# SwiGLU blocks of a two-layer trunk: seven block products moved from the down projection to gate and up, and the down projection's products placed among those of the next chunks

## The chip, the core and the metric

The kernel runs on one core of a Trainium2 chip. TensorE (PE) multiplies into PSUM; VectorE (DVE) and ScalarE (ACT) do the elementwise work and read PSUM; GpSimd (POOL) here issues the DMAs that add to what lies in SBUF; SP issues the plain loads. The metric is the device time of one execution in microseconds. The kernel before takes 2116.01 us, the median of three runs (2115.99 to 2117.65).

## The reference, cut to what matters

The program is a decoder trunk of two layers for 512 tokens and a model width of 1024, in float32. Each layer has a SwiGLU half-step, a group of four mixers between an input and an output projection, a second SwiGLU half-step and a per-layer embedding (PLE) gate.

```python
def swiglu(x, w_gate, w_up, w_down):
    return (jax.nn.silu(x @ w_gate) * (x @ w_up)) @ w_down
...
for l in range(DEPTH):                       # DEPTH = 2, D_MODEL = 1024, D_FF = 2816, SEQ = 512
    h = h + 0.5 * swiglu(rmsnorm(h, ffn1_norm[l]), ffn1_w_gate[l], ffn1_w_up[l], ffn1_w_down[l])
    z = rmsnorm(h, mix_norm[l]) @ w_in[l]
    ...
    h = h + jnp.concatenate([y_a, y_b, y_c, y_d], axis=-1) @ w_out[l]
    h = h + 0.5 * swiglu(rmsnorm(h, ffn2_norm[l]), ffn2_w_gate[l], ffn2_w_up[l], ffn2_w_down[l])
    h = h + (p[l] @ ple_w_proj[l]) * jax.nn.sigmoid(rmsnorm(h, ple_norm[l]) @ ple_w_gate[l])
```

So there are four SwiGLU blocks. The change lies in them and in the stages that feed them.

## The kernel before, in words

**Layout.** Everything is held transposed: the residual `h` is 8 tiles of 128 features by 512 tokens (T), and a product's result has its output features on the 128 partitions. The hidden width 2816 is 22 chunks of 128. The weights lie in HBM so that the 8 blocks (128x128) of one output chunk are one row of 1024 columns.

**Products in float32.** Each float32 operand is split into a high part, rounded to the format fp32r, and a low part, the remainder. `parts` (L133) does it: ACT writes the high part, DVE subtracts. `weights` (L138) loads a row of 1024 columns and splits it; `split` (L201) splits an activation, with the norm's gain as a factor where there is one. `mm3` (L177) then does three matmuls for each 128x128 block: high by high, high by low, low by high. All large products go through it, so their matmuls have the lines L179 to L181 and are told apart by the tile they write.

**Norms.** `Norm.add` (L269) takes one finished tile of `h`: it splits gain times `h` into `x[k]` and adds the squares to `acc`. The row factor r = 1/sqrt(mean square) is made later by `scale` (L282) and multiplied in after the products, so that matmuls can begin before r is there.

**A SwiGLU block** is `ffn` (L296). `hidden` (L304) computes one chunk: the gate's and the up projection's product, each of 8 blocks by 512 tokens (48 matmuls for both, tiles `gu`), then g = silu(gate r) times up times r/2. The 22 chunks come in groups, `PARTS = (8, 8, 6)` (L50).

After each group of 8 comes `down7` (L322), which multiplies the group's 8 chunks by the down weights in the manner of Winograd's form of Strassen's method. The 8 output tiles are 4 pairs (i, i + 4); for each pair the left side is 2x2 (two output tiles by two halves of four chunks) and the right side 2x2 (two halves of four chunks by two halves of 256 tokens). Seven products of four 128x128 blocks by 256 tokens take the place of eight. The right-hand combinations are the tiles `hb1` to `hb4`, made as the chunks come. The left-hand ones are made by `seven` (L149) for each pair: four plain loads on SP's queue and two loads on POOL's queue that add to what the first brought (L163, L164), two sums on DVE (L168, L171), and seven splits of 512 columns. The results stand in the PSUM tiles `dx`, `dy` and `dz` and are added to `h` piece by piece (L365). The order of the 28 products is written out by hand (L368).

The last 6 chunks of a block are multiplied plainly (L384 to L388, tiles `dn`), output tile by output tile, and each finished tile goes to the next norm by `done`.

**Order and buffers.** A scheduler orders each engine's instructions by priority and readiness; work under `urgent` stands far ahead of its place in the program, which is how weights are loaded and split ahead of use. Buffers are slots of a tag: 6 of split weights (`w`), 3 of raw rows (`raw`), 4 of `side` (the sums in `seven`), 4 of `st`, 6 of `t` (temporaries of 128x512), 24 of `u` (pairs of 128x512), and in PSUM 4 `d` (`dense`) and 4 `m` (`mps`).

**The start.** The first chunk's weights and `x` come in pieces (L1060 to L1068), the second chunk's weights in halves (L1070 to L1079); the products of the first chunk are made as the pieces land.

**The stages ahead of a block.** The mixers' output projection (L953 to L960, tiles `y`) and PLE (`ple`, L962, tiles `pg` and `pp`) finish the tiles of `h` in the order 0 to 7 and hand each to `Norm.add`.

## Time and profile before

| | |
|---|---|
| median of three runs | 2116.01 us (2115.99 to 2117.65) |
| the profiled execution, its own time | 2118.98 us |
| its span, first to last instruction | 2117.2 us |
| mean granted TensorE clock | 0.997 |
| moved by DMA | 224.66 MB, 106 GB/s on average |

Where PE's time lies, by the tile that the matmuls write (groups by form, first of the three lines of `mm3`):

| tile | what | matmuls per line | columns |
|---|---|---|---|
| gu | gate and up | 1408 | 512 |
| dx, dy, dz | seven-product downs | 512, 256, 128 | 256 |
| dn | plain downs | 192 | 512 |
| z, n | input projection | 320, 128 | 512 |
| y | output projection | 128 | 512 |
| pg | PLE's gate | 96 and 64 | 512 and 256 |

How to read it: matmuls are pipelined, and the duration of one as the trace gives it (391 ns for 512 columns) is longer than the time from its start to the next one's start. What a matmul costs when PE is full is the length of a window divided by the number of matmuls in it. In the tables of windows the columns are the length, then for each engine its busy time and in brackets the number of its instructions, then the granted clock, the busy share of the DMA engines and GB/s; instructions that reach over an edge are counted in. A line of groups gives line, engine, operation, tiles, shapes and count, then the busy time and the mean ns of one, then the engine's idle time ahead of them and what ended it.

The blocks lie in the trace as follows: the first from 8.5 to 377 us, the second from 652.6 to 1007.3, the third from 1062.5 to 1416.6, the fourth from 1692.1 to 2046.5. Within the first, gate and up of chunks 0 to 7 end at 110.7, the first `down7` at 151.3, chunks 8 to 15 at 238.3, the second `down7` at 278.9, chunks 16 to 21 at 344.2.

### The profile page before, as it was taken

Reading aid. Unit: us, or ns where it says so; the run is one execution under the profiler, and the core shown is the slowest. Engines: PE = TensorE matmul, PEld = TensorE weight load, DVE = VectorE, ACT = ScalarE, POOL = GpSimd, SP = SyncE. Lnnn points to the kernel's source line nnn. Section 1 sums busy time; section 2 is a strip of 40 time slices with the busy share of each in tenths; the row PEclk is TensorE's granted clock in tenths of the full one; section 3 lists DMA queues with packets and bytes.
Section 4 is the critical chain, followed back from the end, with each engine's and each line's share of the span. In section 5 each row is a group of like instructions: output and inputs, shape, how many; then the busy total and the mean of one; then the engine's idle time right before and its main releaser. Section 6 shows DMA issues by size and latency. Waiting matters only on the chain.

```text
span 2117.2 us, 30818 instructions
## 1 busy us (share of the span) xinstructions
PE 2090.1 (99%) x12392; PEld 1755.5 (83%) x12392; DVE 1387.9 (66%) x2286; ACT 883.6 (42%) x1379; POOL 77.0 (4%) x109
## 2 busy tenths in 40 slices
PE   7999999999999999999999999999999999999997
PEld 5898988877788898988888989888777888889887
DVE  5695845786675675845767567467866658566476
ACT  5333423625644333424544333345445434243352
POOL 0010100001000000100000000000010000000000
PEclk9999999999999999999999999999999999999999
DMA  5353423322232453533234434232222335433241
GB/s 183 105 155 118 120 100 90 100 77 79 70 105 95 116 143 100 148 109 92 100 104 134 127 109 115 83 106 93 66 90 72 103 98 137 123 103 116 84 129 50
DMA packets 79376, 224.66 MB, mean 106 GB/s; under 512 B 9472, under 2 KB 13056, under 8 KB 79232
## 3 DMA queue, kind: packets, MB, share of 16 engines
q1 hardware_dynamic: 66320, 200.98, 29.1%
q0 software_dynamic: 10240, 18.88, 5.8%
q10 hardware_dynamic: 2672, 2.82, 0.4%
q8 instruction: 97, 1.59, 0.3%
q14 instruction: 47, 0.39, 0.1%
HBM read 218.45 MB, written 2.10 MB: 104 GB/s over the span
## 4 chain that ended last, share of the span: by engine, by line
PE 93%; DVE 3%; ACT 1%; DMA 1%; issue 1%; SPq 0%; DVEq 0%; ACTq 0%; POOLq 0%
PE gu L179 15%; PE gu L180 15%; PE gu L181 15%; PE z L179 3%; PE z L180 3%; PE z L181 3%; PE dx L179 3%; PE dx L180 3%; PE dx L181 3%; PE dn L179 2%; PE dn L180 2%; PE dn L181 2%; PE dy L181 1%; PE dy L179 1%; PE dy L180 1%; PE y L179 1%
## 5 line engine op out<-in xcount | busy, mean ns | idle before, releaser
L134 ACT CAST wh<-wr 128x1024 fp32r<-128x1024 f32 (+3 forms) x307 | 307.9, 1004 | 717.4 <-issue 330.7
L179 PE MATMUL gu<-x,wh 128*128 128x512 f32 x1408 | 550.3, 391 | 9.9 <-ACT wh L134 3.6
L180 PE MATMUL gu<-x,wh 128*128 128x512 f32 x1408 | 550.4, 391 | 0.0
L181 PE MATMUL gu<-x,wl 128*128 128x512 f32 x1408 | 550.0, 391 | 0.0
L135 DVE TENSOR_TENSOR wl<-wr,wh 128x1024 fp32r<-128x1024 f32 (+3 forms) x307 | 356.8, 1163 | 57.8 <-ACT wh L134 53.8
L179 PEld LDWEIGHTS gu<-x,wh 128*128 128x128 f32 x1408 | 265.7, 189 | 67.4 <-ACT wh L134 4.9
L180 PEld LDWEIGHTS gu<-x,wh 128*128 128x128 f32 x1408 | 265.9, 189 | 55.6 <-DVE x L209 0.6
L181 PEld LDWEIGHTS gu<-x,wl 128*128 128x128 f32 x1408 | 265.8, 189 | 55.0
L317 DVE TENSOR_TENSOR g<-g,gu 128x512 f32<-128x512 f32 x88 | 60.4, 688 | 256.9 <-PE gu L181 251.8
L179 PE MATMUL dx<-hb,ws 128*128 128x256 f32 x512 | 144.2, 285 | 0.3 <-ACT hb L134 0.3
L180 PE MATMUL dx<-hb,ws 128*128 128x256 f32 x512 | 144.3, 283 | 0.0
L181 PE MATMUL dx<-hb,ws 128*128 128x256 f32 x512 | 144.2, 283 | 0.0
L134 ACT CAST ws<-wr 128x512 fp32r<-128x512 f32 x128 | 78.5, 619 | 138.3 <-PE dx L181 84.5
L315 DVE TENSOR_TENSOR g<-gu,r 128x512 f32<-128x512 f32 x88 | 60.6, 689 | 103.0 <-PE gu L181 102.9
L179 PE MATMUL z<-x,wh 128*128 128x512 f32 x320 | 127.7, 399 | 0.0
L180 PE MATMUL z<-x,wh 128*128 128x512 f32 x320 | 126.6, 396 | 0.0
L181 PE MATMUL z<-x,wl 128*128 128x512 f32 x320 | 126.1, 394 | 0.0
L179 PEld LDWEIGHTS dx<-hb,ws 128*128 128x128 f32 x512 | 97.4, 191 | 2.0 <-ACT hb L134 0.5
L180 PEld LDWEIGHTS dx<-hb,ws 128*128 128x128 f32 x512 | 98.0, 191 | 0.3
L181 PEld LDWEIGHTS dx<-hb,ws 128*128 128x128 f32 x512 | 98.1, 192 | 0.0
L134 ACT CAST hb<-g 128x256 fp32r<-128x256 f32 (+1 forms) x128 | 58.8, 459 | 93.6 <-DVE g L318 45.1
L135 DVE TENSOR_TENSOR ws<-wr,ws 128x512 fp32r<-128x512 f32 x128 | 87.5, 689 | 11.4 <-ACT ws L134 11.2
(358 smaller groups left out, 3638.2 us busy)
## 6 DMA issues: line engine op xcount, KB each, us to landing
wr<-in_wgu SPq DMA_DIRECT2D x172, 512.0 KB, 3.2
wr<-in_winT SPq DMA_DIRECT2D x40, 512.0 KB, 3.2
s<-in_wdn SPq DMA_DIRECT2D x64, 256.0 KB, 3.8
s<-in_wdn POOLq DMA_DIRECT2D x64, 256.0 KB, 4.2
wr<-in_wdn SPq DMA_DIRECT2D x32, 512.0 KB, 3.6
wr<-in_wdn SPq DMA_DIRECT2D x32, 384.0 KB, 3.1
a<-in_wdn SPq DMA_DIRECT2D x32, 256.0 KB, 4.7
wr<-in_winN SPq DMA_DIRECT2D x16, 512.0 KB, 3.3
```

What stands on the lines that cost most here:

```text
L134: i = act.copy(hi, src)
L135: dve.tensor_tensor(lo, src, hi.bitcast(F32), op=ALU.subtract)
L179: i = pe.matmul(o, lhsT=a[0], rhs=b[0], start=start, stop=False, skip_group_check=go_on)
L180: pe.matmul(o, lhsT=a[0], rhs=b[1], start=False, stop=False, skip_group_check=go_on)
L181: pe.matmul(o, lhsT=a[1], rhs=b[0], start=False, stop=stop, skip_group_check=go_on)
L315: dve.tensor_tensor(g, ps[0], r, op=ALU.mult)
L317: dve.tensor_tensor(g, g, ps[1], op=ALU.mult)
```

## The change

**Gate and up** of a chunk are now one 2x2 by 2x2 product by seven: the left side is gate and up (two output tiles) by two halves of four blocks of the model width, the right side two halves of the model width by two halves of 256 tokens (`A`, `B`). The class `Chunk` holds it: 7 products of 4 blocks, 84 matmuls of 256 columns. The sums of products stand in two PSUM tiles, X (`gx`, half used) and yz (`gy`); ACT copies X out after products 1, 6 and 7, and `end` puts the pieces together: add, times r, silu, times up, times -r/2, split. `seven` serves it with the same loads, sums and splits as before, the splits in another order.

**The order** of products is by hand: 1 and 5 of a chunk, then 4 of the chunk before, 6, 3 of the chunk before with its `end`, then 2 and 7. Down products stand between them.

**The right side** is made once per block by the class `Right`, from pairs of tiles (k, k + 4) of gain times `h`, through `Norm.add7`. For this the output projection and PLE (of the first layer) finish their tiles in the order 0, 4, 1, 5, 2, 6, 3, 7 (`PAIRED`), and PLE's projection weights are loaded for each tile alone (256 columns) and not in fours.

**Down** products are all plain: `PARTS` is (4, 4, 4, 4, 6). A group's downs run among the products of the next group, a step (one output tile, 12 matmuls of 512 columns) at a time, from that group's second chunk on; weights come two tiles in a row of 1024. The last 6 chunks' downs stand at the end as before.

**The first block** keeps its first two chunks plain, since their products begin before all of `h` is there. Its right side uses `x[k]` as made for these (`plain`); the loads for chunk 2 stand behind those of the constants on SP's queue, and its splits for products 7, 4 and 3 behind the norm's Exp on ACT.

```diff
-PARTS = (8, 8, 6)
+PARTS = (4, 4, 4, 4, 6)
...
+    PAIRED = [m + e * KD // 2 for m in range(KD // 2) for e in range(2)]
...
+            dst = raw.rearrange("p (m c) -> p m c", m=2) if two else raw[:, :cols]
+            nc.sync.dma_start(out=dst, in_=src)
...
-    def seven(a1, a2):
+    def seven(a1, a2, wait=None, late=None):
...
+            inturn(nc.sync.dma_start(out=s1, in_=a2[:, 0:T]), wait)
+            inturn(nc.sync.dma_start(out=s3, in_=a1[:, 0:T]), wait)
+            inturn(nc.sync.dma_start(out=raw, in_=a1), wait)
             nc.gpsimd.dma_start(out=s1, in_=a2[:, T:WB], accum_op=ALU.add)
             nc.gpsimd.dma_start(out=s3, in_=a2[:, 0:T], accum_op=ALU.add)
-            nc.sync.dma_start(out=a22, in_=a2[:, T:WB])
+            inturn(nc.sync.dma_start(out=a22, in_=a2[:, T:WB]), wait)
             keep(1, r1, 0)
             keep(5, s1, 0)
             dve.tensor_tensor(r1, r1, s1, op=ALU.add)
+            keep(6, r1)
             keep(2, r2)
-            keep(6, r1)
+            for p, src in ((7, s3), (4, a22)):
+                inturn(keep(p, src), late)
             dve.tensor_tensor(r2, r2, r1, op=ALU.add)
-            keep(3, r2)
-            keep(7, s3)
-            keep(4, a22)
+            inturn(keep(3, r2), late)
         return w
...
+    class Right:
+        def __init__(self, plain=None):
+            self.f = {}
+            self.plain = plain
+            self.b4 = None
+        def put(self, p, x, c0):
+            self.f.setdefault(p, []).append(xpart(x, c0, H))
+        def add(self, j, g1, g2):
+            if self.plain is None:
+                b1, b2 = unit(F32R, name="b1"), unit(F32R, name="b2")
+                parts(b1[:, 0, A], b1[:, 1, A], g1[:, A])
+                t1, c1 = b1, H
+            else:
+                b1, b2 = self.plain[j], self.plain[j + 4]
+                if j % 2 == 0:
+                    self.b1 = unit(F32R, name="b1")
+                t1, c1 = self.b1, j % 2 * H
+            dve.tensor_tensor(g1[:, A], g1[:, A], g1[:, B], op=ALU.subtract)
+            parts(t1[:, 0, c1:c1 + H], t1[:, 1, c1:c1 + H], g1[:, A])
+            if self.plain is None:
+                parts(b2[:, 0], b2[:, 1], g2)
+            dve.tensor_tensor(g1[:, B], g2[:, B], g1[:, B], op=ALU.subtract)
+            dve.scalar_tensor_tensor(g1[:, A], g1[:, A], -1.0, g2[:, B], op0=ALU.mult, op1=ALU.subtract)
+            b3 = unit(F32R, name="b3")
+            parts(b3[:, 0], b3[:, 1], g1)
+            dve.scalar_tensor_tensor(g2[:, A], g1[:, A], -1.0, g2[:, A], op0=ALU.mult, op1=ALU.subtract)
+            if j % 2 == 0:
+                self.b4 = unit(F32R, name="b4")
+            c = j % 2 * H
+            parts(self.b4[:, 0, c:c + H], self.b4[:, 1, c:c + H], g2[:, A])
+            for p, x, c0 in ((1, b1, 0), (5, t1, c1), (2, b2, 0), (3, b2, H), (6, b3, 0), (7, b3, H), (4, self.b4, c)):
+                self.put(p, x, c0)
...
+        def add7(self, k, plain=None):
+            g = t2(name="xg")
+            act.activation(g, h[k], AF.Copy, scale=gain(self.gi, k))
+            if plain is None:
+                self.square(k)
+            if k < KD // 2:
+                if k == 0:
+                    self.right = Right(plain)
+                self.g1 = g
+            else:
+                self.right.add(k - KD // 2, self.g1, g)
...
-        def hidden(f, g):
-            ps = []
...
-        def down7(f0):
...
+        def product(o, w, p, first):
+            for j in range(KD // 2):
+                mm3(o, (w[p][:, 0, j * P:j * P + P], w[p][:, 1, j * P:j * P + P]), norm.right.f[p][j],
+                    first and j == 0, j == KD // 2 - 1, True)
+        class Chunk:
+            def __init__(self, f):
+                late = norm.exp if start and f == 2 else None
+                self.w = seven(wgu[idx, f, 0], wgu[idx, f, 1], start and start[1], late)
+                X, yz = dense("gx"), dense("gy")
+                self.X, self.yz = X[:, A], yz
+                self.c, self.u = t2(name="g"), t2(name="u")
+                self.go(1)
+                self.go(5)
+            def go(self, p):
+                o = {2: self.yz[:, A], 5: self.yz[:, B], 3: self.yz[:, B]}.get(p, self.X)
+                product(o, self.w, p, p in (1, 5))
+                with urgent():
+                    if p == 1:
+                        act.copy(self.c[:, A], o)
+                    elif p == 6:
+                        act.copy(self.c[:, B], o)
+                    elif p == 7:
+                        act.copy(self.u[:, B], o)
+                        dve.tensor_tensor(self.u[:, B], self.u[:, B], self.yz[:, B], op=ALU.add)
+            def end(self):
+                g = self.c
+                dve.tensor_tensor(g, g, self.yz, op=ALU.add)
+                dve.tensor_tensor(g, g, r, op=ALU.mult)
+                act.activation(g, g, AF.Silu)
+                dve.tensor_tensor(g[:, A], g[:, A], self.X, op=ALU.mult)
+                dve.tensor_tensor(g[:, B], g[:, B], self.u[:, B], op=ALU.mult)
+                dve.tensor_tensor(g, g, rn, op=ALU.mult)
+                hid.append(split(g, name="hid"))
+        def down(m, f0, hs, w, c0):
+            n = len(hs)
+            o = mps("dn")
+            for f in range(n):
+                mm3(o, wpart(w, c0 + f * P), xpart(hs[f]), f == 0, f == n - 1)
+            dve.tensor_tensor(h[m], h[m], o, op=ALU.add)
+        def downs(f0, hs):
+            for m in range(0, KD, 2):
+                w = weights(wdn[idx, m:m + 2, :, f0 * P:(f0 + 4) * P].rearrange("m p c -> p m c"), two=True)
+                for e in range(2):
+                    yield down(m + e, f0, hs, w, e * T)
+        def step():
+            for d in todo[:1]:
+                if next(d, 0) == 0:
+                    todo.pop(0)
...
+                q = Chunk(f)
+                last = f == NF - 1
+                if i:
+                    step()
+                if prev:
+                    prev.go(4)
+                q.go(6)
+                if prev:
+                    prev.go(3)
+                    prev.end()
+                if last:
+                    q.go(7)
+                    q.go(2)
+                else:
+                    q.go(2)
+                    if i:
+                        step()
+                    q.go(7)
+                    if i and n == 4:
+                        step()
+                prev = q
+                if f == 9 and hook is not None:
+                    hook()
+                if i == 0 and g:
+                    todo.append(downs(f0 - PARTS[g - 1], hid[:PARTS[g - 1]]))
+                    del hid[:PARTS[g - 1]]
             f0 += n
+        prev.go(4)
+        prev.go(3)
+        prev.end()
+        while todo:
+            step()
+        n = PARTS[-1]
+        f0 = NF - n
+        for m in range(KD):
+            w = weights(wdn[idx, m, :, f0 * P:NF * P], n * P)
+            down(m, f0, hid, w, 0)
+            done(m)
...
-        for m in range(KD):
+        for m in PAIRED:
...
-            for m in range(KD):
-                if m % 4 == 0:
-                    wpj = weights(wpp[l, :, m // 4 * WB:(m // 4 + 1) * WB])
-                chunk(m, weights(wpg[l, m]), wpj)
+            for m in PAIRED:
+                wpj = weights(wpp[l, :, 2 * m * P:2 * (m + 1) * P], 2 * P, one=True)
+                chunk(m, weights(wpg[l, m]), wpj, 0)
...
+    start[1] = inturn(nc.sync.dma_start(out=cs, in_=cst[:, 0:K_TOP]), prev)
+    for k in PAIRED:
+        norm.add7(k, norm.x)
...
-        mixers(l, norm, nxt.add)
+        mixers(l, norm, nxt.add7)
-            ple(l, norm, nxt.add)
+            ple(l, norm, nxt.add7)
```

More of the change, by code (lines that the diff above doesn't have):

```diff
@@ L999, in ple @@
         for m in range(KD // 2):
-            chunk(m, weights(wpg[l, m]), wpj)
+            chunk(m, weights(wpg[l, m]), wpj, 2 * m)
             if m == 0:
@@ L1021, in ple @@
             for m in range(KD // 2, KD):
-                last = chunk(m, ws[m - KD // 2], wpj, c0, n)
+                last = chunk(m, ws[m - KD // 2], wpj, m % 4 * 2, c0, n)
                 if c0 and m == KD // 2:
@@ L1069, in trunk @@
     nextw = []
+    start = [first, None, nextw]
     with urgent():
```

130 lines of the change are left out of this document (36 added, 94 removed).

## The prediction

> **What bounds the kernel now.** First the page's engine shares, then the windows, cut where the kind of matmul changes.
>
> ```profile
> span 2117.2 us, 30818 instructions
> PE 2090.1 (99%) x12392; PEld 1755.5 (83%) x12392; DVE 1387.9 (66%) x2286; ACT 883.6 (42%) x1379; POOL 77.0 (4%) x109
> ```
> ```profile
> core 0: us, PE busy (x) PEld busy (x) DVE busy (x) ACT busy (x) POOL busy (x), PEclk, DMA share, GB/s
> 30.00:40.00 10.00, 10.00 (x45) 7.99 (x44) 3.47 (x6) 3.05 (x6) 0.00 (x0) 1.00 0.32 107
> 40.00:50.00 10.00, 6.63 (x23) 5.03 (x22) 7.78 (x13) 4.92 (x7) 0.00 (x0) 0.83 0.17 52
> 110.70:151.30 40.60, 40.60 (x338) 40.44 (x337) 39.71 (x81) 17.25 (x27) 5.25 (x6) 1.00 0.58 145
> 151.30:238.30 87.00, 87.00 (x386) 72.05 (x385) 58.05 (x94) 31.90 (x49) 2.59 (x3) 1.00 0.41 125
> 238.30:278.90 40.60, 40.60 (x337) 40.43 (x337) 32.30 (x62) 16.63 (x26) 3.64 (x4) 1.00 0.36 100
> 344.20:377.00 32.80, 32.80 (x145) 26.95 (x144) 23.18 (x31) 16.16 (x23) 0.00 (x0) 1.00 0.34 105
> 608.80:652.60 43.80, 43.80 (x193) 35.89 (x192) 27.11 (x34) 18.61 (x26) 0.00 (x0) 1.00 0.31 103
> 1016.30:1062.50 46.20, 46.20 (x205) 38.25 (x204) 33.79 (x45) 21.43 (x30) 0.00 (x0) 1.00 0.30 101
> ```
>
> TensorE is the bound, and it does not wait: in the SwiGLU blocks the PE column equals the window. A busy PE need not be at its peak, so I take its pace from the counts. The gate and up window 151.3 to 238.3 is 8 chunks of 48 matmuls (2 products x 8 blocks x 3): 87.0 / 384 = 226.6 ns for a matmul of 512 columns. The window 238.3 to 278.9 is one group of seven-product downs, 7 x 4 pairs x 4 blocks x 3 = 336: 40.6 / 336 = 120.8 ns for 256 columns, with the weight load busy throughout (40.43). The last downs (344.2 to 377.0, 8 x 6 x 3 = 144) take 227.8 ns. So half the columns cost 53% of the time: seven products in place of eight save not 12.5% but 1 - 84 x 120.8 / (48 x 226.6) = 6.7%.
>
> What stands behind PE is DVE: 32.3 to 39.7 us of 40.6 in the seven-product windows, 27.1 of 43.8 in the output projection (608.8), 33.8 of 46.2 in the PLE stage (1016.3).
>
> **PE's own sum.** Before, a SwiGLU block costs 22 x 48 x 226.6 ns = 239.3 us of gate and up, 2 x 40.6 = 81.2 of seven-product downs and 32.8 of plain ones: 353.3 us. After: 22 chunks x 84 x 120.8 ns = 223.2, and plain downs of 22 x 8 x 3 = 528 matmuls at 226.6 = 119.6: 342.8 us, so -10.5. In the first block two chunks stay plain (+0.73 each), -9.0. Four blocks: -9.0 - 3 x 10.5 = -40.5 us, made of about 63 us gained on gate and up and 23 lost on downs. The trace has both matmul forms, so this term is known to a few us. In the last PLE stage 256-column matmuls run a little closer:
>
> ```profile
> 2079.33 0.28 PE L180 MATMUL pg<-x,wk 128*128 128x256 f32 x1
> ...
> 2079.93 0.28 PE L179 MATMUL pg<-x,wk 128*128 128x256 f32 x1
> ```
>
> Five steps from start to start (four lines are left out) take 0.60 us, 120 ns each. By that pace a block's gate and up is 1.5 us less, four blocks 5.8, and the sum about -46; as the seven-product windows are this very form, I keep 120.8.
>
> The Trainium skill ("TensorE: Matmul & The Clock Gate", section "Back-to-back issue gap") gives a warm matmul N / 2.4 + 2.5 ns: 109.2 and 215.8 ns as estimates. By that the sum would be about -64 us. Both rows here lie 11 ns higher, and a fixed cost weighs double on the halved matmul, so the measurement decides and I give the -64 no chance.
>
> **What DVE and ACT get.** Rows for each piece:
>
> ```profile
> L135 DVE TENSOR_TENSOR wl<-wr,wh 128x1024 fp32r<-128x1024 f32 x261 | 319.0, 1222 | 56.7 <-ACT wh L134 52.9 <-PE n L181 2.6
> L135 DVE TENSOR_TENSOR ws<-wr,ws 128x512 fp32r<-128x512 f32 x128 | 87.5, 689 | 11.4 <-ACT ws L134 11.2
> L318 DVE TENSOR_TENSOR g<-g,rh 128x512 f32<-128x512 f32 x88 | 60.7, 691 | 2.3
> L982 DVE TENSOR_TENSOR pg<-pg,r 128x512 f32<-128x512 f32 x12 | 8.3, 692 | 8.1 <-PE pg L181 8.1
> L365 DVE TENSOR_TENSOR h<-h,dx 128x256 f32<-128x256 f32 x128 | 52.6, 420 | 35.2 <-PE dx L181 34.0
> L209 DVE SCALAR_TENSOR_TENSOR x<-h,vec,x 128x512 fp32r<-128x512 f32 x64 | 47.7, 747 | 19.0 <-ACT x L208 10.9 <-DMA wr<-in_wgu 8.1
> L168 DVE TENSOR_TENSOR wr<-wr,s 128x512 f32<-128x512 f32 x32 | 22.0, 688 | 0.0
> L388 DVE TENSOR_TENSOR h<-h,dn 128x512 f32<-128x512 f32 x32 | 22.0, 687 | 33.5 <-PE dn L181 33.5
> ```
> ```profile
> L134 ACT CAST wh<-wr 128x1024 fp32r<-128x1024 f32 x261 | 274.6, 1052 | 630.4 <-issue 275.2 <-PE gu L180 187.4 <-PE z L180 62.9
> L134 ACT CAST ws<-wr 128x512 fp32r<-128x512 f32 x128 | 78.5, 619 | 138.3 <-PE dx L181 84.5 <-PE dy L181 20.8 <-PE gu L180 15.3
> L316 ACT ACTIVATE g<-g 128x512 f32<-128x512 f32 x88 | 55.2, 628 | 1.5 <-DVE g L315 0.4
> L208 ACT ACTIVATE x<-h,vec 128x512 fp32r<-128x512 f32 x64 | 46.1, 721 | 25.4 <-DVE h L985 14.3 <-DMA h<-in_xT 9.8
> L983 ACT ACTIVATE pg<-pg 128x512 f32<-128x512 f32 x12 | 7.5, 627 | 5.0 <-DVE pg L982 5.0
> L134 ACT CAST hb<-g 128x256 fp32r<-128x256 f32 x96 | 38.9, 406 | 70.6 <-DVE g L331 45.0 <-DVE g L318 22.1 <-DVE g L341 3.5
> ```
> ```profile
> 30.04 0.69 DVE L280 TENSOR_TENSOR acc<-acc,sq 128x512 f32<-128x512 f32 x1
> 35.20 1.23 DVE L135 TENSOR_TENSOR wl<-wr,wh 128x1024 fp32r<-128x1024 f32 x1 [4.47 <-ACT wh L134]
> ...
> 41.23 0.69 DVE L227 SCALAR_TENSOR_TENSOR r<-rt,r 128x512 f32<-128x512 f32 x1
> ...
> 42.98 1.28 DVE L315 TENSOR_TENSOR g<-gu,r 128x512 f32<-128x512 f32 x2
> ```
>
> A gate and up chunk now needs on DVE: seven split subtractions and two weight sums, 9 x 0.69 = 6.2 us; the chunk's end, four operations of 512 columns (add yz, times r, times rn, split of hid) and three of 256, 4 x 0.69 + 3 x 0.42 = 4.0. That is 10.2 us against 84 x 120.8 ns = 10.15 of PE. ACT: 7 x 0.62 + 3 x 0.41 + 2 x 0.63 = 6.8 us, no bound. A group of downs adds 4 x 1.22 + 8 x 0.69 = 10.4 us of DVE to 8 x 4 x 3 x 226.6 ns = 21.8 of PE, so four chunks with a group of downs are 51.2 us of DVE in 62.4 of PE, and the last six chunks 71.6 in 82.7. There DVE has slack.
>
> The thin place is the start of each block. Group 0 and the first chunk of group 1 have no downs beside them: five chunks at 10.2 us of DVE for 10.15 of PE. But means overstate DVE: the last timeline row has two such operations in 1.28 us, so independent ones follow at about 0.6, and 10.2 comes to about 9.2. Before, the window at 110.7 ran DVE at 39.71 of 40.60 with PE full, and a seven-product down pair is much the same load (6.2 + 7 x 0.42 = 9.1 per 10.15). So I expect short stalls, not a new bound.
>
> Added at the start is the right-hand side: per pair of h blocks, DVE has five operations of 256 columns (three combinations, splits of t1 and b4) and one of 512 (b3), plus b1's 256 and b2's 512 outside the first block, with one more combination: 7 x 0.42 + 2 x 0.69 = 4.3 us, 17 per block in place of 8 x 0.75 = 6.0. The output projection goes from 27.1 to about 38 of 43.8 us of DVE: covered. PLE goes from 33.8 of 46.2 to about 44: barely. If that cover fails, the same 11 us per block is the price.
>
> **Stalls, term by term.** (a) First block. r was ready at 41.9 us (L227 in the timeline above), and PE stood in the 40 to 50 window:
>
> ```profile
> PE gu L179 <- ACT wh L134: 3.6, 2, 3.1
> PE gu L179 <- DVE g L315: 3.4, 1, 3.4
> PE gu L179 <- ACT x L208: 3.0, 1, 3.0
> ```
>
> That stays: chunk 2 still needs a bank that waits for g times r. That bank came when the first of L315's pair ended, at about 43.7, and three chunks and two products (3 x 10.15 + 2.9) later, at 77, the first down comes. DVE, free from 31 on by the timeline, has until then: about 13 us of right-hand side, four sevens (25), the ends of chunks 0 to 3 (15), norm (4): 57 us for 46, about 50 at the close pace. Bounds 0 and 12; I take 4, by the close pace. (b) Blocks two and four: from the last h to b3 is an add, the scaled copy, two combinations and the split, 0.69 + 0.72 + 0.84 + 1.31 = 3.6 us and hops, against products 1 and 5 (24 x 120.8 ns = 2.9 us) which need only h[3]. Bounds 0 to 6, I take 2 each. (c) Block three, after PLE: the gate's three multiplications and sigmoid stand ahead, about 6.5 us; 5, with bounds 0 to 11. (d) Ends of blocks: the last hid follows add, r, silu, product, rn and split, 4.6 us, where five blocks of the first down cover 15 x 226.6 ns = 3.4: bounds 0 to 2 each, I take 0.5, so 2. Sum 15 us; all lower bounds 0 (PE has no idle there to give back), all upper ones 12 + 12 + 11 + 8 = 43.
>
> **Waits and queues that are added.** Product 6 now waits for ACT's copy of X after product 1, 7 for the one after 6, and the chunk's 4 for the one after 7. Each copy is 0.41 us, with two other products (2.9 us) between; behind it on ACT stand the next splits, at 6.8 of 10 us no press. In the first block chunk 2's loads come after the constants on SP, and three of its splits behind the norm's Exp on ACT; PE cannot start that chunk before r in any case. Nothing for either, and the bank rival's price if DVE or ACT hold them up.
>
> Two accumulating DMAs per chunk go to POOL's queue, 172 in place of 64:
>
> ```profile
> s<-in_wdn POOLq DMA_DIRECT2D x64, 256.0 KB, 4.2
> L163 POOL DMA_DIRECT2D s<-in_wdn x32 | 28.4, 888 | 1126.7 <-ACT hb L134 794.3 <-ACT pt L874 104.6 <-ACT g L316 90.4
> ```
>
> POOL: 2 x 0.89 us per 10 us chunk, issue to landing 4.2 us, while a chunk's buffers are asked for one chunk ahead. On SP's queue a chunk's plain loads stand before the next step's down weights; the 238.3 window, one seven per 10 us, used 0.36 of the DMA engines. Nothing.
>
> **Forecast.** -40.5 + 15 = -25 us. The profiled execution took 2118.98 us (span 2117.2 and 1.8 around it), 3.0 above the median 2116.01: 2094 by its measure, 2091 by the median's.
>
> **Rivals.** *No stalls*: the close pace of DVE and the full PE at 39.71 of 40.60 speak for it. 2116 - 40 = 2076. Chance 0.25. The forecast, 2080 to 2100 (stalls of 5 to 25): 0.42.
>
> *DVE becomes the bound of the first five chunks*: stalls of 25 to 43 us, all upper bounds; 2100 to 2118, 2110 near the middle. For it: the 40 to 50 window shows PE's granted clock fall to 0.83 with one stall, so that a stall costs more than its length. Against it: PE full in every seven-product window. Chance 0.17.
>
> *Slower: banks come free late in every chunk.* X and yz have two slots each. Chunk f+2 cannot start before X of f is multiplied in: add, r, silu, product, 0.69 + 0.69 + 0.63 + 0.42 = 2.4 us, and hops, after product 3. Cover without a down step is two products, 2.9 us. Weight splits marked urgent stand ahead on DVE's in-order queue, and if one waits there for its accumulating DMA (4.2 us) or a buffer, bank and PE wait behind it. It decides from 40.5 / 86 = 0.47 us per chunk; at 0.7 the cost is 60, and the time 2136. Against it: the seven-product downs ran on the same buffers at the same pace. Chance 0.13.
>
> *The accumulations get late*: POOL builds descriptors while DVE is busy. If each came 1 us too late for PE, 86 us against 40.5, 2161. The Trainium skill ("SBUF — State Buffer", the "DVE blocks DMA" trap) says that DVE's two-port modes lock GpSimd out; no delay shows here beside a DVE busy 98%, with 888 ns per issue on average. Chance 0.03.
>
> **Numbers.** A measurement of this kernel tells about 0.2%, 4.2 us, from no change. Faster by more: 0.25 + 0.42 + 0.13 of the DVE case = 0.80; within: 0.04 of that and 0.04 of the last two, 0.08; slower 0.12, the rest of those two. The range runs from the PE sum at 120 ns (2070) and a little noise, 2069, to 2114 in the upper part of the DVE case, and leaves out the rest of that and the last two rivals, under 0.2.
>
> **What would show.** Right: products gx and gy at about 121 ns, 84 per chunk; downs at 227; PE idle of 10 to 20 us more, at the blocks' starts, put down to ACT b3 or DVE; DVE near 80% of the span. Wrong: PE waiting on g or c in most chunks (the banks), on s1 or s3 (the accumulations), a granted clock below 1 inside blocks, or a pace of mixed 256 and 512 matmuls off 120.8 and 226.6.

## The result and the profile after

The changed kernel takes 2146.39 us (median of four runs, 2144.37 to 2147.1); the kernel before took 2116.59 beside it (four runs, 2115.99 to 2117.65). The ratio is 1.0139, 95% interval 1.0121 to 1.0156: slower by 30 us where 25 us of gain were forecast. The profiled execution took 2146.84 us. First its page, then its windows (columns as for before), cut at the places that the prediction named.

```profile
span 2145.1 us, 36254 instructions
PE 2078.9 (97%) x14336; PEld 1821.7 (85%) x14336; DVE 1599.0 (75%) x2720; ACT 1061.8 (50%) x1897; POOL 171.1 (8%) x217
```
```profile
core 0: us, PE busy (x) PEld busy (x) DVE busy (x) ACT busy (x) POOL busy (x), PEclk, DMA share, GB/s
28.50:46.50 18.00, 2.01 (x5) 0.60 (x3) 17.64 (x40) 12.89 (x27) 1.78 (x3) 0.58 0.38 86
46.50:50.00 3.50, 3.50 (x16) 3.50 (x17) 2.62 (x5) 3.28 (x6) 0.82 (x1) 0.50 0.60 93
146.50:230.90 84.40, 70.60 (x433) 64.49 (x432) 62.89 (x110) 30.66 (x57) 11.58 (x13) 0.88 0.58 148
162.40:192.30 29.90, 16.10 (x86) 15.19 (x85) 25.20 (x49) 8.99 (x16) 5.77 (x7) 0.71 0.60 129
366.20:398.50 32.30, 32.22 (x143) 26.36 (x142) 24.48 (x34) 15.86 (x23) 0.00 (x0) 1.00 0.39 117
630.40:674.20 43.80, 43.80 (x194) 35.91 (x193) 38.13 (x65) 27.65 (x48) 2.51 (x3) 1.00 0.40 113
674.20:734.80 60.60, 56.89 (x457) 55.20 (x455) 49.01 (x86) 37.81 (x72) 7.88 (x10) 1.00 0.60 153
700.00:715.00 15.00, 13.29 (x110) 13.29 (x111) 14.41 (x26) 10.99 (x22) 3.49 (x4) 1.00 0.70 152
734.80:798.10 63.30, 63.30 (x434) 58.46 (x433) 46.71 (x76) 28.41 (x53) 6.96 (x8) 1.00 0.57 150
1032.90:1084.30 51.40, 51.34 (x227) 42.13 (x226) 44.66 (x78) 32.63 (x58) 2.62 (x3) 1.00 0.39 115
```

Three places leave PE idle: the wait for the norm in the first block (28.5 to 46.5, and 3.5 us at half clock behind it, 16 matmuls of 256 columns at 219 ns each), a group of the first block (146.5 to 230.9, idle in 162.4 to 192.3), and the start of the second block, from its first product to its first down (674.2 to 734.8). Where the second block's start is thinnest, DVE is nearly full (14.41 of 15.00 us from 700). The steady group at 734.8, four chunks with a group of downs, is full: 63.3 us where 336 x 120.8 + 96 x 226.6 ns = 62.3 were reckoned. The output projection (43.8) is as long as before. From the end of one block to the start of the next it is 55.3 us around PLE (before 55.2) and 275.7 around the mixers (before 275.6), so the whole difference lies in the blocks. (They are 30.7 us longer together and the profiled executions differ by 27.9, mostly because the first product starts at 5.2 us in place of 8.5.) The waits of PE (engine and tile that waited, what ended the wait; us in all, times, longest):

```profile
PE ms L247 <- ACT ac L243: 9.2, 1, 9.2
PE gx L190 <- ACT g L389: 9.1, 2, 8.2
PE gx L190 <- ACT u L393: 7.4, 9, 1.8
PE gx L190 <- DVE g L435: 6.6, 1, 6.6
PE gy L190 <- DVE g L398: 4.1, 3, 1.9
PE gx L190 <- DVE g L398: 3.8, 1, 3.8
```

Idle time tells only half. PE's busy time fell by 11.2 us (2090.1 to 2078.9), though the new products should take 40 us less. So each step from a matmul's start to the next one's was compared with its full-speed length (120.6 ns for 256 columns, 226.6 for 512), within the four blocks. What is over, in us:

| | before | after | tables kept apart | and plain starts |
|---|---|---|---|---|
| full-speed sum of the blocks | 1410.8 | 1370.7 | 1370.7 | 1375.2 |
| steps too long by over 60 ns: first block | 15.5 | 42.9 | 21.9 | 19.4 |
| the same, blocks two to four | 4.2 | 26.5 | 28.0 | 5.6 |
| late first and later steps of downs | 0.4 | 22.6 | 20.2 | 20.7 |
| all other steps | -0.4 | -1.2 | -1.0 | -0.9 |
| the blocks together | 1430.7 | 1461.4 | 1439.7 | 1420.1 |

The two columns on the right are two of the experiments below; the profiled execution of the last was its fastest, 3.5 us under its median. The full-speed sum fell by 40.1 us; the late steps rose by 71 us.

### The profile page after: what moved, and what is told of

Same layout as the page of the kernel before. It is cut to its first block, busy times and chain, and to the rows that moved or that the text cites. A ratio compares the mean times of both kernels' runs of the same rounds, so it can differ in the third digit from the quotient of the medians.

```text
span 2145.1 us, 36254 instructions
## 1 busy us (share of the span) xinstructions
PE 2078.9 (97%) x14336; PEld 1821.7 (85%) x14336; DVE 1599.0 (75%) x2720; ACT 1061.8 (50%) x1897; POOL 171.1 (8%) x217
## 4 chain that ended last, share of the span: by engine, by line
PE 87%; DVE 6%; DMA 3%; ACT 3%; issue 1%; SPq 0%; ACTq 0%; DVEq 0%
PE dn L190 8%; PE dn L192 7%; PE gx L190 7%; PE gx L192 7%; PE gx L191 7%; PE dn L191 7%; PE gy L190 5%; PE gy L191 5%; PE gy L192 5%; PE z L190 3%; PE z L191 3%; PE z L192 3%; DMA wr<-in_wgu 1%; PE y L190 1%; PE y L192 1%; PE y L191 1%
## 5 line engine op out<-in xcount | busy, mean ns | idle before, releaser
L190 PE MATMUL gx<-b,ws 128*128 128x256 f32 x1296 | 368.7, 285 | 19.2 <-ACT g L389 9.1
L191 PE MATMUL gx<-b,ws 128*128 128x256 f32 x1296 | 367.3, 283 | 0.0
L192 PE MATMUL gx<-b,ws 128*128 128x256 f32 x1296 | 367.1, 283 | 0.0
L139 DVE TENSOR_TENSOR ws<-wr,ws 128x512 fp32r<-128x512 f32 x344 | 233.9, 688 | 134.3 <-ACT ws L138 133.7
L139 DVE TENSOR_TENSOR wl<-wr,wh 128x1024 fp32r<-128x1024 f32 (+3 forms) x197 | 222.4, 1131 | 149.0 <-PE gy L192 78.9
L190 PE MATMUL dn<-hid,wh 128*128 128x512 f32 x704 | 281.0, 399 | 0.9 <-ACT wh L138 0.5
L192 PE MATMUL dn<-hid,wl 128*128 128x512 f32 x704 | 279.3, 398 | 0.0
L191 PE MATMUL dn<-hid,wh 128*128 128x512 f32 x704 | 275.0, 392 | 0.0
L190 PEld LDWEIGHTS gx<-b,ws 128*128 128x128 f32 x1296 | 248.8, 192 | 27.0 <-ACT u L393 10.0
L190 PE MATMUL gy<-b,ws 128*128 128x256 f32 x872 | 249.3, 286 | 5.4 <-DVE g L398 4.1
L191 PEld LDWEIGHTS gx<-b,ws 128*128 128x128 f32 x1296 | 248.8, 192 | 3.5
L191 PE MATMUL gy<-b,ws 128*128 128x256 f32 x872 | 248.0, 284 | 1.7 <-DVE b L139 1.7
L192 PEld LDWEIGHTS gx<-b,ws 128*128 128x128 f32 x1296 | 248.8, 192 | 0.1
L192 PE MATMUL gy<-b,ws 128*128 128x256 f32 x872 | 247.1, 284 | 1.3 <-DVE ws L139 1.3
L190 PEld LDWEIGHTS gy<-b,ws 128*128 128x128 f32 x872 | 168.4, 193 | 8.0 <-DVE g L398 4.7
L191 PEld LDWEIGHTS gy<-b,ws 128*128 128x128 f32 x872 | 168.5, 193 | 3.3 <-DVE b L139 1.9
L192 PEld LDWEIGHTS gy<-b,ws 128*128 128x128 f32 x872 | 168.1, 193 | 2.9 <-DVE ws L139 1.5
L192 PEld LDWEIGHTS dn<-hid,wl 128*128 128x128 f32 x704 | 132.3, 188 | 34.4 <-DVE wl L139 3.3
L190 PEld LDWEIGHTS dn<-hid,wh 128*128 128x128 f32 x704 | 132.8, 189 | 33.1 <-ACT wh L138 8.1
L191 PEld LDWEIGHTS dn<-hid,wh 128*128 128x128 f32 x704 | 132.9, 189 | 24.9
```

Source lines behind the costliest of these rows:

```text
L139: dve.tensor_tensor(lo, src, hi.bitcast(F32), op=ALU.subtract)
L190: i = pe.matmul(o, lhsT=a[0], rhs=b[0], start=start, stop=False, skip_group_check=go_on)
L191: pe.matmul(o, lhsT=a[0], rhs=b[1], start=False, stop=False, skip_group_check=go_on)
L192: pe.matmul(o, lhsT=a[1], rhs=b[0], start=False, stop=stop, skip_group_check=go_on)
```

## The experiments

All ran in three rounds or more beside the kernel before; the ratio to it is given with its interval.

**The group at 146.5: the rotary tables.** `tables`, called once by the hook at chunk 9, computes sines and loads factors into six shared slots `t`. ACT's timeline shows what it does to the chunks (start, duration, in brackets the idle time ahead and what ended it):

```profile
183.35 0.63 ACT L501 ACTIVATE si<-ang 128x512 f32<-128x512 f32 x1 [2.90 <-DVE ang L500]
183.38 0.82 ACTq L513 DMA_DIRECT2D dec<-in_dec  x2
184.24 0.47 ACTq L519 DMA_DIRECT2D masks<-in_cst  x1
189.13 0.37 ACT L389 COPY g<-gx 128x256 f32<-128x256 f32 x1 [5.15 <-DVE tabsq L516]
```

and DVE's, what let ACT go on:

```profile
187.81 0.69 DVE L516 TENSOR_TENSOR tabcq<-co,dec 128x512 f32<-128x512 f32 x1 [4.54 <-DMA dec<-in_dec]
188.41 0.69 DVE L516 TENSOR_TENSOR tabsq<-si,dec 128x512 f32<-128x512 f32 x1
```

The tables' loads are issued only at 183.4, after the sine `si` has been let go on the same queue. The queue has done with them at 184.7, and ACT still stands: its copy of product 1 begins when DVE's product `tabsq` has read `dec`, the tables' factor, and the two have nothing in common but the slot `t` that `dec` lay in and the copy's tile `g` takes. PE waits 8.2 us for the copy. In all PE is idle for 13.8 us in this group; the rest of the loss goes with the granted clock, 0.71 from 162.4 to 192.3. Three runs: the tables moved behind the block, two more slots, and the tables' temporaries in tiles of their own.

```diff
-                if f == 9 and hook is not None:
-                    hook()
...
+        if l == 0:
+            tables()
```

> The changed kernel, with the rotary tables made after the first block instead of beside its tenth chunk. Both theories say that the tables cost the first block about 21 us there (its third group takes 84.4 us, the same groups of the second block 63.2). So about 2125, if the tables find room beside the mixers' input projection; 2146 would say that the long group has another cause.

Measured: 2146.55 us, 1.014 (1.0121 to 1.0159). In the profiled execution (2153.25 us, the slowest of four) the first block fell from 393.3 to 374.8 us, but the mixers behind it took 294.4 in place of 275.7. The cost moved along with the tables.

```diff
-        return up.tile(list(shape), dt, tag="u", bufs=24, name=nm(name))
+        return up.tile(list(shape), dt, tag="u", bufs=23, name=nm(name))
...
-        return tp.tile(list(shape), dt, tag="t", bufs=6, name=nm(name))
+        return tp.tile(list(shape), dt, tag="t", bufs=8, name=nm(name))
```

> The changed kernel with 8 slots for temporaries of 128x512 in place of 6, and 23 of pairs in place of 24. Theory (slots): a22 of each seven-product load, c and u of each chunk and the passing temporaries share 6 slots, and a late a22 or a full pool stops ACT in its order, with the PSUM banks behind it. Then the third group of block one loses most of its 21 us and the blocks' starts half of their 7 to 11 us: 2105 to 2118. Rival (DVE throughput at those places): 2140 to 2150, since DVE's work is the same.

Measured: 2146.91, 1.0137 (1.0122 to 1.0152). The first block fell to 389.3 only, and the others rose by as much. Two slots more, with one `u` fewer, are not enough.

```diff
-        pin = t2((P, T), I32, name="pin")
-        posf = side(name="posf")
...
+        tm, cq, sq_, ck, sk = (cp.tile([P, T], F32, name=f"tab{n}") for n in ("M", "cq", "sq", "ck", "sk"))
+        nc.scalar.dma_start(out=cq.bitcast(I32), in_=pos)
...
-            a, n = t2(name="ang"), t2(name="turn")
+            n = ck
...
-        co, si = t2(name="co"), t2(name="si")
```

> The changed kernel, tables at the same place, their intermediate values kept in the tables' own tiles, so that only two passing temporaries take a slot of t. The same operations on DVE and ACT. Theory (slots): 12 to 20 us less than the changed kernel, 2126 to 2134. Rival (DVE throughput): within 4 us of 2146.

Measured: 2126.0, 1.0035 (1.0021 to 1.005), 20 us less than the changed kernel with the same operations. Its windows of the same group and of the second block's start:

```profile
145.30:208.40 63.10, 63.10 (x433) 58.55 (x432) 48.03 (x79) 28.71 (x54) 6.91 (x8) 1.00 0.58 157
652.30:715.70 63.40, 58.43 (x458) 56.71 (x456) 49.30 (x86) 38.06 (x72) 8.12 (x10) 0.97 0.58 146
```

The group is 63.1 us, full, in place of 84.4. So the tables' hold on the slots cost 21 us, and not their work: they now use two slots `t` in passing, and the last of their loads is issued at 154.9 where it was 184.2. The edit also takes the tables' tile `posf` out of one of the four slots `side`, which the chunks' sums use; what each kind of slot cost is not separated. The start of the second block is as thin as before. This kernel is the base of what follows.

**Plain downs by themselves.** The kernel before, with every group of downs plain:

```diff
-            if n == 8:
+            if n == 80:
                 down7(f0)
...
-                done(m)
+                if f0 + n == NF:
+                    done(m)
```

> The kernel before with its seven-product downs made plain, nothing else. By the pace of matmuls (120.8 and 226.6 ns) each of 8 groups goes from 40.6 to 43.5 us: 23 us more, 2139. If the loss of the plain downs is less than that because the seven-product downs have a cost beside their matmuls, 2116 to 2130.

Measured: 2138.04, 1.0094 (1.0079 to 1.0109), 20.4 us more. The prediction's loss on downs was 23: that term held (blocks two to four are 5.4 to 5.9 us longer each, the first 0.9).

**The starts of blocks two to four.** From the first product to the first down these take 60.3 to 63.6 us with 456 matmuls, 55.1 at 120.8 ns. Which shared thing is it: the load of `a22` that ACT waits for, the buffers of raw rows or split weights, the norm, the speed of DVE, or the order of the work?

```diff
+            inturn(nc.sync.dma_start(out=a22, in_=a2[:, T:WB]), wait)
             inturn(nc.sync.dma_start(out=raw, in_=a1), wait)
...
-            inturn(nc.sync.dma_start(out=a22, in_=a2[:, T:WB]), wait)
```

> On the version whose tables take no slots (2126.0 us): the load of a22 issued ahead of the 512 KB row and not behind it. At the start of block two ACT stands 5.0 us for a22, whose load was issued at 672.87, just behind a row that had waited for its buffer, and PE waits 2.4 us behind ACT. Theory (order of loads): blocks two and four start 2 to 5 us shorter (63.4 and 60.5 us from the block's start to its first down product now), 2116 to 2122 in all. Rival (DVE throughput, 97% busy there): the wait moves to another operation, 2124 to 2128.

Measured: 2131.9, 1.0062 (1.0044 to 1.008). Starts of 64.3, 63.6 and 63.3 us, where the base has 63.4, 63.5 and 60.4: no shorter. The load was not the limit.

```diff
-            dve.tensor_tensor(r1, r1, s1, op=ALU.add)
+            pool.tensor_tensor(r1, r1, s1, op=ALU.add)
...
-            dve.tensor_tensor(r2, r2, r1, op=ALU.add)
+            pool.tensor_tensor(r2, r2, r1, op=ALU.add)
```

> On the version whose tables take no slots (2126.0 us): the two weight sums of each chunk on POOL in place of DVE, 1.4 us of 10.2 less for DVE per chunk. Rival theory (DVE throughput): five chunks at each block's start gain up to 1.4 each, 5 us per block, 2106 to 2114. Theory (late loads and the order behind them): POOL is slower than DVE at a sum and has the accumulating loads queued behind it, so the splits of products 6 and 3 and the rows' buffers come later: 2124 to 2140.

Measured: 2167.2, 1.023 (1.0211 to 1.0249). A group of POOL (busy us and mean ns behind the bar) shows why this says little of DVE:

```profile
L184 POOL TENSOR_TENSOR wr<-wr 128x512 f32<-128x512 f32 x86 | 137.3, 1597 | 151.0 <-DVE ws L139 149.8 <-DMA masks<-in_cst 1.2
```

A sum takes 1597 ns there, 685 on DVE, in a chain that the splits wait for. Two more runs gave one buffer more, each in place of one `u`:

```diff
-        return wp.tile([P, WB], F32, tag="raw", bufs=3, name=nm("wr"))
+        return wp.tile([P, WB], F32, tag="raw", bufs=4, name=nm("wr"))
```

> On the version whose tables take no slots (2126.0 us): 4 buffers for raw rows in place of 3, 23 of pairs in place of 24. If rows wait for a buffer and ACT for rows (191 us of ACT's idle time in the changed kernel ends with such a row), each block's start loses 3 to 6 us and the whole 10 to 20: 2106 to 2116. If DVE's throughput or the split weights' buffers bound, within 3 us of 2126.

```diff
-        return wp.tile([P, WB], F32R, tag="w", bufs=6, name=nm(name))
+        return wp.tile([P, WB], F32R, tag="w", bufs=7, name=nm(name))
```

> On the version whose tables take no slots (2126.0 us): 7 buffers for split weights in place of 6, 23 of pairs in place of 24. A chunk takes five, and products 4 and 3 of the chunk before hold theirs into the next one. If that sets when rows come free, 2108 to 2118; if DVE's throughput bounds the starts, within 3 us of 2126.

Measured: 2143.39, 1.0121 (1.0105 to 1.0137), and 2153.27, 1.0167 (1.014 to 1.0195). Both were slower, and since no run takes the one `u` away alone, what the added buffer did by itself is not shown. The starts with the seventh `w` (60.2, 62.1, 58.6) look shorter, but their first down comes after 444 matmuls and not 456, which is 1.4 us; the blocks grew (359.1, 362.6, 359.2 against 357.5, 358.4, 353.9).

```diff
             def end(self):
+                with urgent():
+                    self.finish()
```

> On the version whose tables take no slots (2126.0 us): a chunk's end (add yz, r, silu, up, rn, split) is marked urgent as the weight splits are, so that it stands ahead of the splits of later chunks on DVE and ACT. Theory (order: splits ahead of the ends keep PSUM banks taken): the waits of PE for g and u at the starts (12 us in all) mostly go, the three starts of 60.5 to 63.5 us become 56 to 59, and the whole 2108 to 2118. Rival (DVE throughput): another operation is late in its place, 2122 to 2130.

Measured: 2123.89, 1.003 (1.002 to 1.004). Starts of 59.0, 62.9 and 59.0: the chunk's end ahead of the splits helps a little. The next leaves out part of the computation: in products 7, 4 and 3 the weights' low part is not made and the high part is read in its place, which takes three subtractions, 2.1 us, from DVE in each chunk.

```diff
+            if p in (7, 4, 3):
+                i = act.copy(w[p][:, 0], src)
+                w[p] = w[p][:, 0:1].to_broadcast([P, 2, T])
+                return i
```

> On the version whose tables take no slots (2126.0 us): leaves out the low parts of the weights of products 7, 4 and 3 (the matmuls stay and read the high part twice), 2.1 of 10.2 us less DVE work per chunk. Rival theory (DVE throughput at the starts): the three starts become 54 to 57 us in place of 60.5 to 63.5 and the first block's gains as much, 2092 to 2108. Theory (order): DVE's relief helps by less than half of that, 2112 to 2122.

Measured: 2123.99, 1.0031 (1.0019 to 1.0043). The window of the second block's start:

```profile
653.70:712.50 58.80, 56.94 (x457) 55.31 (x455) 38.80 (x69) 37.43 (x72) 7.77 (x9) 1.00 0.65 159
```

DVE has 20 us to spare there (38.80 of 58.80), and the start is still 3.8 us over its 55.1; the starts together got 8 us shorter, the whole 2. DVE's speed is a part of it and not the whole.

```diff
-                if start and f < 2:
+                if f < 2:
...
-        mixers(l, norm, nxt.add7)
+        mixers(l, norm, nxt.add_both)
```

> On the version whose tables take no slots (2126.0 us): the first two chunks of every block are plain, as they are in the first block. Price by the pace of matmuls: 2 x 0.73 us in three blocks, 4.4 us. If the thin place is the five chunks without downs, three are left and each of these starts loses 3 to 6 us net, 2110 to 2120. If the cost lies with the right-hand side or is spread over the block, 2126 to 2134.

(`add_both` makes both the plain tiles and the seven-product side.) Measured: 2108.94 us (2105.46 to 2109.64), 0.9957 (0.9942 to 0.9972): faster than both kernels. The start of the second block:

```profile
649.40:706.40 57.00, 56.99 (x385) 52.50 (x383) 44.55 (x74) 35.08 (x61) 6.89 (x8) 1.00 0.54 139
```

PE is full. Two plain chunks cost 1.5 us of PE in each block, and the late steps of blocks two to four fell from 28.0 to 5.6 us. A plain chunk asks for 48 matmuls of 226.6 ns with two splits of 1024 columns: more of PE's time for less of everyone else's. The edit changes more than one thing, though: these chunks also need none of the seven-product right side and no copies of X, and which of this ended the stalls is not separated.

```diff
         r = norm.scale()
+        if start:
+            for k in PAIRED:
+                norm.add7(k, norm.x)
...
-    for k in PAIRED:
-        norm.add7(k, norm.x)
```

> On the version whose tables take no slots (2126.0 us): the first block's right-hand side comes after the norm's factor in the program and not ahead of it. PE stands 18 us there, 9.3 for the norm's sum behind ACT and 6.7 for r. If the right-hand side's temporaries and DVE work hold up r, r comes 4 to 10 us sooner: 2116 to 2122. If chunk 2 then waits as long for its right-hand side, 2124 to 2128.

Measured: 2124.81, 1.0035 (1.0022 to 1.0048), on the base with the tables apart. The first block's two waits of 9.3 and 6.7 us became one of 14.5. Same place, same price.

**The late downs.** In the changed kernel 81 of the 136 switches from products to a down begin with a step of 213 to 270 ns (one of 813) where 55 take 120, and the 81 steps behind them take 334 ns or more in place of 233. One of them, on DVE, on PE and on PE's weight loads:

```profile
735.90 1.23 DVE L139 TENSOR_TENSOR wl<-wr,wh 128x1024 fp32r<-128x1024 f32 x1 [2.31 <-PE gy L192]
```
```profile
736.97 0.28 PE L192 MATMUL gy<-b,ws 128*128 128x256 f32 x1
...
737.18 0.50 PE L192 MATMUL dn<-hid,wl 128*128 128x512 f32 x1
...
737.52 0.39 PE L190 MATMUL dn<-hid,wh 128*128 128x512 f32 x1
```
```profile
736.85 0.19 PEld L192 LDWEIGHTS gy<-b,ws 128*128 128x128 f32 x1
737.18 0.19 PEld L192 LDWEIGHTS dn<-hid,wl 128*128 128x128 f32 x1
```

The split ends at 737.13, and the matmul that reads it starts at 737.18. PE waited, and the profile shows no gap, since the modelled end of the matmul ahead (736.97 + 0.28) lies behind that start. So it is at 80 of the 81: the down starts 0.05 or 0.06 us after its split ends. And in 60 of the 81, as here (2.31 us), the split was not held up by other work: its engine stood idle until 0.08 or 0.09 us after the last matmul of a product, 36 times in `gx` and 24 in `gy`. What the two share is a slot `w`, which the product's weights held and the row takes; of the six a chunk takes five and a row of down weights two. Is it the number of slots, or the order? The split weights of these downs in tiles of their own (the pool `u`), on the base, then with plain starts, then with urgent ends too:

```diff
-                w = weights(wdn[idx, m:m + 2, :, f0 * P:(f0 + 4) * P].rearrange("m p c -> p m c"), two=True)
+                w = weights(wdn[idx, m:m + 2, :, f0 * P:(f0 + 4) * P].rearrange("m p c -> p m c"), two=True, keep=True)
```

> On the version whose tables take no slots (2126.0 us): the split weights of the down products that stand among the next chunks lie in two of the 24 pairs of 128x512 and not in two of the six buffers of split weights. Theory (down weights late for want of a buffer): the 79 late switches to down products and the 89 late second matmuls, 20 us in all, go to under a third, 2106 to 2114. Rival (the switch from 256 to 512 columns costs PE that much by itself): they stay, 2122 to 2130.

> On the version with two plain chunks at each block's start (2108.9 us): the same move of the down products' split weights. If the two causes are apart, the 20 us of late switches go here too: 2089 to 2097, faster than both kernels. If the pairs run short, since the plain start keeps two more of them, 2100 to 2112.

> The version before with the chunk's end marked urgent as well. With two plain chunks the starts have hardly a wait of PE left, so within 3 us of that version; 3 to 6 us less if ends behind splits still hold PSUM banks inside the groups.

Measured: 2166.1, 1.0231 (1.0211 to 1.0251); 2155.3, 1.0176 (1.0153 to 1.0198); 2135.46, 1.0079 (1.0064 to 1.0094). Each is slower than the same without the edit, and the wait is now plain to see in the first of them:

```profile
PE dn L190 <- ACT wk L138: 15.5, 34, 1.8
```

The edit was not the clean test that it was meant to be: 14 of the 24 `u` hold the right side and 8 hold `hid`, so two are left, one row of down weights. Where a row was split too late here, its load had been issued at 1850.76, the last reader of the row before it had started at 1858.56, and ACT split it at 1864.83, right behind a chunk's `hid`:

```profile
1864.31 0.62 ACT L216 CAST hid<-g 128x512 fp32r<-128x512 f32 x1 [1.34 <-DVE g L403]
1864.83 1.04 ACT L138 CAST wk<-wr 128x1024 fp32r<-128x1024 f32 x1
```

So it is in 39 of the 43 late switches of this run: neither load nor slot was last, which leaves the order. The run with a seventh `w` says the same of the shared slots: 74 switches are late in it. Next, each row asked for one step earlier, with plain starts, first in the shared slots, then in tiles of its own:

```diff
-            for m in range(0, KD, 2):
-                w = weights(wdn[idx, m:m + 2, :, f0 * P:(f0 + 4) * P].rearrange("m p c -> p m c"), two=True)
-                for e in range(2):
-                    yield down(m + e, f0, hs, w, e * T)
+            def row(m):
+                return weights(wdn[idx, m:m + 2, :, f0 * P:(f0 + 4) * P].rearrange("m p c -> p m c"), two=True)
+            def run(w):
+                for m in range(0, KD, 2):
+                    yield down(m, f0, hs, w, 0)
+                    w1, w = w, row(m + 2) if m + 2 < KD else None
+                    yield down(m + 1, f0, hs, w1, T)
+            return run(row(0))
```

> The version with two plain chunks at the start of every block (2108.9 us), with each row of down weights made one step earlier: a group's first row when the chunk ahead of the group's downs ends, and every further row ahead of the second of the two steps that use the row before it. Buffers stay shared, six slots of w. Theory 'the splits of the down weights stand too late in the order of ACT and DVE': the late switches to dn (81 of 136 begin at 226 or 264 ns instead of 120, and 98 second steps at 335 instead of 227, together 20.8 us) nearly vanish, and the time falls by 10 to 20 us to 2089 to 2099. Rival 'the slots of w are the limit, whatever the order': a row that is asked for earlier takes its two slots earlier, and those are missing for the chunk's own splits; the time stays within 4 us or rises by up to 20, and PE gets new waits for gx or gy.

Measured: 2112.45, 0.9973 (0.9963 to 0.9983), against 0.9957 without the edit: no gain. But the late switches fell from 79 to 16, with the same slots, and none of the 16 waits for weights (their splits had ended 9 us before), so it is how late a row is asked for that makes its weights late. The waits of PE show what came in their place:

```profile
PE dn L190 <- ACT hid L216: 8.2, 12, 1.4
...
PE dn L191 <- DVE hid L217: 3.9, 14, 0.3
```

With weights ready sooner, the scheduler put the downs forward (the second block's first one comes 54.5 us after its start in place of 57.0), and there they wait 12.1 us for the last `hid` of their group. The late steps of the downs are 21.4 us in all where they were 20.7: late weights were exchanged for late `hid`.

> As the run before it, but with the down weights of the interleaved steps in tiles of their own instead of slots of w (that version stood at 2155.3 us without the earlier row, with 21.6 us of PE's waits for ACT's split wk in 39 places). Theory 'order': with the row asked for a step earlier, these waits go and the time falls by 20 us or more, below 2135. Theory 'both order and slots': it falls below the run beside it, towards 2090. Rival 'the load itself is late, since raw's three slots are in turn with those of the chunks': the time stays at 2145 to 2160, and PE's waits for wk stay above 15 us.

Measured: 2141.2, 1.0103 (1.008 to 1.0126): 14 us better than own tiles without the earlier row, still worse than shared slots, with 17.5 us of waits for `wk` in 30 places. Last, plain starts with urgent ends:

> The version with two plain chunks at the start of every block (2108.9 us), with Chunk.end under urgent, which gained 2.1 us where the starts were not plain and 19.8 us where the down weights were apart. If what it does is to bring chunk ends ahead of splits on DVE, the gain comes in the steady groups too: 2105 to 2107. Rival: it helped only at the starts, which are plain now: 2108 to 2110.

Measured: 2111.62, 0.9968 (0.9955 to 0.998): no gain over plain starts alone. So the urgent end helped at the starts, which are plain now. An order in which neither weights nor `hid` come late was not found; whether there is one stays open.

## Why the prediction was wrong

The first table closes the account. Forecast and result differ by 56 us in the blocks (-25 against +30.7).

- **PE's own sum: right.** -40.5 forecast, -40.1 by the steps counted. Plain downs cost 20.4 us where 23 were reckoned, and the steady group shown runs 1.0 us over its sum.
- **The tables: the step that failed most, 21 us.** "What DVE and ACT get" counted chunks, downs and the right-hand side. It left out what the hook at chunk 9 puts into the first block, though the code shows it there before and after. Before, the same work stood in the 87.0 us of gate and up, with PE full and DVE at 58.05. The new chunks hold `t` slots for `g`, `u` and `a22` across two chunks and need ACT between products. The experiment that took the tables out of the slots gave 20 us back.
- **"Short stalls, not a new bound" at the starts: right in place, wrong in size, 16 us, and in the terms.** Blocks two to four: 9 us were taken, for the right side and PLE's gate (b, c); late steps rose from 4.2 to 26.5. The first block is 6.4 us worse by the table, 4 taken. What came was not what had been priced: of the 12.6 us for which PE stood idle in these three starts, 2.8 ended on the right side or PLE's gate, all in block three, and 9.4 on ACT's copies of X (L389, L391, L393) or on DVE's add that frees yz (L398), as did 3.7 later in these blocks. For the copies the prediction had "Nothing for either". DVE's speed was the smaller part: with 2.1 us less per chunk the starts kept 14 of the 22 us of excess that the base has. Plain first chunks removed most of it; that seven-product chunks without downs leave ACT, DVE and the banks too little time beside PE is the likely reason, not a shown one.
- **"There DVE has slack", the down weights at "Nothing": the third failed step, 20 us.** DVE had slack (46.71 of 63.3), and the splits still came late: the prediction counted DVE's time, and not when a row gets its two slots of `w`. In 60 of 81 cases the split began only when a product had let go of the slot, and the down met its weights some 0.1 us late. The argument that the seven-product downs "ran on the same buffers" overlooked that chunks and rows of down weights now share the six slots at one time. (Of the 22.6 us in the table's row 19.7 are at the 81 switches, 1.2 fall in the tables' group at half clock, and 1.4 are the waits for a block's last `hid`, for which term (d) had taken 2: that one held.)
- **Rivals.** DVE as the whole of it fell with the run that took work from it. Late accumulations fell as a cause: an issue took 891 and 879 ns on POOL against 888 before; a landing took 4.9 us in the median against 4.2, and PE waited for the split of such a sum in one place of weight, 1.9 us in the tables' group. Nearest came the bank rival, with its 2136: at the starts PE did wait for the copies and for yz. But it was to strike in every chunk at 0.7 us; a steady chunk loses a quarter of a microsecond, and at the downs' weights, not at the banks.
- **The range** ended at 2114, inside the upper bounds of the four stalls. The two costs that the sum left at zero, tables and down weights, had no bound at all, and they made some 41 of the 56 us.

The groups that bear the last points, of the changed kernel: the splits of the down weights, with what their wait ended on, and the accumulating loads.

```profile
L139 DVE TENSOR_TENSOR wl<-wr,wh 128x1024 fp32r<-128x1024 f32 x151 | 184.8, 1224 | 140.2 <-PE gy L192 72.6 <-ACT wh L138 33.7 <-ACT g L391 29.8
L174 POOL DMA_DIRECT2D s<-in_wgu x86 | 76.6, 891 | 635.4 <-DMA s<-in_wgu 149.0 <-DVE wl L139 141.5 <-DVE ws L139 138.6
L175 POOL DMA_DIRECT2D s<-in_wgu x86 | 75.6, 879 | 794.7 <-DVE ws L139 189.1 <-DMA s<-in_wgu 180.3 <-DVE h L411 173.8
```

## What to carry to other kernels

A change that makes the bounding engine's work shorter must be costed against everything that runs beside it, one-off work in a hook included: list what holds the shared buffers and who queues behind it. Slack of an engine over a stretch is no proof that each of its results is there in time; ask for every operand on the path where its maker stands in the queue and whose slot it takes. Where a faster form starves at the start of a stage, keep the slow form for the first pieces: with the tables apart, two plain chunks per block turned a loss of 0.4% into a gain of 0.4%.

## What was not expected of the hardware

- A PE that the profile shows as busy lost some 20 us in pieces of 0.1 us: 10.6 in the 81 late first steps and 9.1 in the steps behind them, whose own operands were there. The late matmul is shown at 0.50 us where the next takes 0.39, and its weight load starts together with it (737.18) where the one before started 0.12 us ahead of its matmul (736.85); that this is what lengthens the second step is not shown. Idle time counts from the modelled end of a matmul (0.28 us after its start for 256 columns), and the next can start 0.12 after it, so a wait below about 0.16 us leaves no gap. Steps from start to start show it.
- The mixed stream costs next to nothing by itself: where weights were there in time, the first 512-column matmul behind a 256-column one started 120 ns after it, the next 233 or 234 ns after that, and the further 512-column steps stayed mostly at 227 ns.
- More buffers were no help where a `u` was given up for them: the run with a fourth raw row took 17 us more, with a seventh split-weight slot 27, with own tiles for the down weights 40, each against the same kernel without it. Whether the lost `u` or another order of the scheduler's did it is not shown.
- The Trainium skill ("TensorE: Matmul & The Clock Gate", section "Back-to-back issue gap") gives N / 2.4 + 2.5 ns as the gap of an isolated warm matmul, which makes 109.2 ns as an estimate for 256 columns. Inside full windows here the steps are 120.0 to 120.8 ns, so the measurement decides again, and a 256-column matmul costs more than half of a 512-column one.
